# The gate ahead of the reciprocal at the end of an attention group, a third buffer of exponentials, and narrower blocks of ones

## The chip, the cores and the metric

The kernel runs on one core of a Trainium2 chip. The metric is the device time of one execution in microseconds (us); lower is better. The engines are named as the profile names them: PE (matmuls; PEld for its weight loads), DVE (vector), ACT (activations, casts), POOL (the general engine) and SP (the queue that issues most DMAs).

## What is computed

Two layers of a diffusion backbone over 1024 latent tokens and 256 context tokens of 1024 channels. The even layer has two attentions of 8 query heads and 2 key heads each: a global one over all 1280 keys, and a windowed one over the context and a band of +-128 latent keys, with a learned sink per head. The odd layer has a convolution module and a neighbourhood attention of 8 heads on the 16x64 grid with a bias table. Every branch is multiplied by a SiLU gate. What matters here is the end of each attention:

```python
p = jax.nn.softmax(s, axis=-1)                       # with the sink as one more column in the windowed one
o = jnp.einsum("bhgqk,bkhd->bqhgd", p.astype(v.dtype), v)
...
y_lat = jnp.concatenate([oa * jax.nn.silu(ag), ob * jax.nn.silu(bg)], axis=-1) @ w_out     # even layer
y_lat = jnp.concatenate([oc, od * jax.nn.silu(dg)], axis=-1) @ w_out                       # odd layer
```

## The kernel before

All products run on PE as three products of parts: each operand is split into a high part (rounded to the type that PE takes in one pass) and a low part (the rest), as high x high, low x high and high x low. `split` (L323) does it: a cast on ACT, a subtraction on POOL or DVE.

**Order of the work.** Both layers weave two streams: `main`, the attention (`attn_gen`, L428), and a filling of projections (`weave`, L533, with fixed numbers of steps of each). The framework then puts every engine's instructions into an order by these priorities and its own estimate of times; on the chip each engine runs its list in order. So a slow step holds whatever stands behind it on its engine.

**Groups.** In the first layer a group is one unit `u` (of four: 4 query heads that share a key head) and one block of 128 queries (`group0`, L595), so 512 columns of queries x heads; units run in the order 2, 3, 0, 1, blocks in the order `QORD` (2, 3, 4, 0, 5, 6, 1, 7, 8, 9). Blocks 0 and 1 are context and have two key tiles of 128; the others have 4 or 5 (windowed units) or 10 (global ones). In the second layer a group is one head and one half of the grid (`group1`, L1376), with seven key tiles. There are 40 and 16 groups and 364 tiles in all.

**A tile** (L488 to L528): PE makes the scores into a bank `st` of PSUM (two buffers; L503, L507), ACT takes the exponentials into `pf` (L515; in the second layer DVE adds the bias first, L512 and L513), `split` makes `ph` (cast, ACT) and `pl` (POOL, every 12th or 5th tile DVE) of it. `pf` has PFB = 2 buffers, in the first layer under the tag `ost`, which some small tiles of the start share; `ph` and `pl` have four each. Up to three tiles later `flush` (L435) multiplies by the values: three products into the bank `ov` of PSUM, which has one buffer. A key block of the value tile `V` holds 192 columns: 64 low parts, 64 high parts, 64 ones. L445 multiplies columns 64 to 192 by `ph`: rows 0 to 63 of `ov` get the values, rows 64 to 127 all get the sum of exponentials. L446 adds the low parts, L447 does columns 64 to 192 with `pl`, and L450 adds the sink.

**The end of a group** (L451 to L459), all on DVE: two transposes of 32x32 blocks bring the sums from rows 64 to 127 of `ov` to partitions (`r1`; of each block only the first row is used later), the reciprocal is taken (`r8`, L457), and a third transpose of a broadcast spreads it over the columns (`rb`, L458). Then `finish`: in the first layer (L665) two multiplies of `ov` by `rb` into `y` (L669), one multiply of `y` by 0.5 and the gate `gt` (L671), then a DMA to `Od` (L674), or for the last unit a split into the operands of the output projection. `y` has one buffer (YB). In the second layer (L1447) the same with L1451, L1453 and a DMA to `O1d`; its `y1` shares a tag of three buffers with the gate. The gate's rows are loaded by `gate` (L605, L1402) when the middle tile of the group is reached. Only when the last read of `ov` is done may L445 of the next group begin.

`V` is filled by DMA from DRAM (L590, L1410), its ones are set once by POOL for each of the two buffers (L582, L379); at the start the same tag serves as a buffer for modulation weights (`mw_tile`, L168).

Of the kernel before, what the change touches and what calls it, by code (L numbers as in the profile page):

```python
# [10 lines left out]
F32 = mybir.dt.float32  # L11
# [27 lines left out]
VSH = 5  # L39
VORD = (1, 2, 0)  # L40
WBN = 8
TRV = "pp"
HALF = {'half': 3, 'hf': 2}
STG = {"pair": 2, "vT": 1, "spo": 2}
# [3 lines left out]
VS0 = 12  # L48
N0 = 9
NLAST = (48, 28)  # L50
PFB = 2
MWB, WRB = 2, 4
OHQ = 0
PCB = 3
# [46 lines left out]
def tile_kernel(ctx: ExitStack, tc: tile.TileContext, a, out):  # L101
# [23 lines left out]
    def nm(s):  # L125
        uid[0] += 1
        return f"{s}_{uid[0]}"
# [40 lines left out]
    def mw_tile():  # L168

        ring = MWR if mwp[0] is not None else "ABAV"  # L170
        mk[0] += 1
        t = ring[mk[0] % len(ring)]
        if t == "x":
            w = mwp[0].tile([P, 1024], F32, tag="mwx", name=nm("mw"), bufs=2)
        else:
            w = a0.tile([P, 1920 if t == "V" else NTOK], F32, tag={"A": "KA", "B": "KB", "V": "V"}[t], name=nm("mw"),
                        bufs=2)
        return w[:, 0:1024].rearrange("p (d n) -> p d n", d=2)

# [8 lines left out]
    def mod_half(pool, l, part, j):  # L188

        pb = bank("pp", nm("pm"))  # L190
        c0 = part * 1024 + j * 512
        for d2 in range(4):
            w2 = mw_tile()
            mm0.append(SY.dma_start(w2, a["mod_w"][l, 2 * d2 * P : (2 * d2 + 2) * P, c0 : c0 + 512].rearrange("(d p) n -> p d n", d=2)))
            for d in range(2):
                dk = 2 * d2 + d
                pmm.append(PE.matmul(pb[0:2, :], csil[:, dk, :], w2[:, d, :], start=(dk == 0), stop=(dk == DK - 1)))
            yield
        row = a0.tile([P, 512], F32, tag="ost", name=nm("mrow"), bufs=2)[0:2, :]
        SC.copy(row, pb[0:2, :])  # L200
        yield
        tr = bank("tr", nm("trm"))
        for i in range(4):
            PE.transpose(tr[:, 2 * i : 2 * i + 2], row[:, i * P : (i + 1) * P], ident[0:2, 0:2])
        trv = tr[:, 0:8].rearrange("p (i c) -> p i c", c=2)
        o = part * 8 + j * 4
        dst = modT[l][:, o : o + 4, :]
        VE.tensor_tensor(dst, trv, modb[:, l, o : o + 4, None].broadcast_to([P, 4, 2]), op=ALU.add)
        if part == 1:
            VE.scalar_tensor_tensor(gs[l][:, j * 4 : j * 4 + 4, :], dst, 1.0,  # L210
                                    normg[:, l, j * 4 : j * 4 + 4, None].broadcast_to([P, 4, 2]),
                                    op0=ALU.add, op1=ALU.mult)
        yield
# [160 lines left out]
    Ks, Vs = [], []  # L374

    def v_tiles(pool, n, bufs=1):
        Vs[:] = [pool.tile([P, n, 192], F32R, tag="V", name=nm("Vt"), bufs=bufs) for _ in range(bufs)]
        for V in Vs:
            GP.memset(V[:, :, 128:192].bitcast(F32), 1.0)  # L379

    def k_tiles(pool, n, bufs=1):
        KA = pool.tile([P, n * P], F32R, tag="KA", name=nm("KAt"), bufs=bufs)
# [42 lines left out]
    def flat(ap, q, n):  # L425
        return ap[:, :n].rearrange("p (r c) -> p r c", c=q[1]) if isinstance(q, tuple) else ap[:, :n]

    def attn_gen(pool, groups, vshare, look, nexts=None):  # L428

        preps = [g.prep for g in groups]  # L430
# [4 lines left out]
        def flush():  # L435
            g, t, ph, pl = pend.pop(0)
            k, q0, n, _ = g.tiles[t]
            if t == 0:
                g.ov = bank("ov", nm("ov"))
                if g.load_v is not None:  # L440
                    g.load_v()
            V = g.v(k)
            last = t == len(g.tiles) - 1
            o, ph, pl = cut(g.ov, q0, n), flat(ph, q0, n), flat(pl, q0, n)
            PE.matmul(o, V[:, 64:192], ph, start=(t == 0), stop=False)  # L445
            PE.matmul(cut(g.ov[0:64], q0, n), V[:, 0:64], ph, start=False, stop=False)  # L446
            pvs.append(PE.matmul(o, V[:, 64:192], pl, start=False, stop=(last and g.sink is None)))  # L447
            if last:
                if g.sink is not None:
                    PE.matmul(g.ov, g.skm(), g.QL[0:76, :], start=False, stop=True)  # L450
                r1 = pool.tile([P, 8, 32], F32, tag="r1", name=nm("r1"), bufs=1)  # L451
                r8 = pool.tile([P, 8], F32, tag="r8", name=nm("r8"), bufs=2)
                rb = pool.tile([P, 256], F32, tag="rb", name=nm("rb"), bufs=1)
                for e in range(2):
                    VE.transpose(r1[e * 64 : (e + 1) * 64].rearrange("p a b -> p (a b)")
                                 .rearrange("p (a q) -> p a q", a=2), g.den(g.ov[64:128, :], e))
                VE.reciprocal(r8, r1[:, :, 0])  # L457
                VE.transpose(rb, r8[:, :, None].broadcast_to([P, 8, 32]))  # L458
                g.finish(g.ov, rb)  # L459

        for p in preps[:2]:
            if not layer[0]:
# [112 lines left out]
    def kv_tiles(u):  # L575

        if not both:
            for _ in range(2):
                both.append((a0.tile([P, NTOK], F32R, tag="KB", name=nm("KBt"), bufs=2),
                             a0.tile([P, 10, 192], F32R, tag="V", name=nm("Vt"), bufs=2)))  # L580
                GP.memset(both[-1][0][64:68, :].bitcast(F32), 1.0)
                GP.memset(both[-1][1][:, :, 128:192].bitcast(F32), 1.0)  # L582
        KAs[u] = a0.tile([P, NTOK], F32R, tag="KA", name=nm("KAt"), bufs=2)
        KBs[u], V0s[u] = both[ORDER.index(u) % 2]

    def load_kv(u, j0, j1):

        ts = slice(j0 * P, j1 * P)
        SY.dma_start(KAs[u][:, ts].bitcast(F32), Kd[u][:, ts])
        SY.dma_start(V0s[u][:, j0:j1, 0:128].bitcast(F32), Vd[u][:, j0:j1])  # L590

    def copy_k(KA, KB):
        SC.copy(KB[0:64, :], KA[0:64, :].bitcast(F32))
# [1 line left out]
    def group0(u, qb):  # L595
# [66 lines left out]
        def den(dn, e):  # L662
            return dn.rearrange("p (e f q) -> p f e q", f=2, e=2)[:, :, e, :]

        def finish(ov, rb):  # L665
            y = a0.tile([P, 2, P], F32, tag="y", name=nm("y"), bufs=YB)
            for e in range(2):
                es = slice(e * 64, (e + 1) * 64)
                VE.tensor_tensor(y[es], den(ov[0:64, :], e), rb[es, :].rearrange("p (a q) -> p a q", a=2),  # L669
                                 op=ALU.mult)  # L670
            VE.scalar_tensor_tensor(y, y, 0.5, g.gt, op0=ALU.mult, op1=ALU.mult)  # L671
            fs, ts = slice(2 * u, 2 * u + 2), slice(qb * P, (qb + 1) * P)
            if u != ORDER[-1]:
                SY.dma_start(Od[:, fs, ts], y)  # L674
            else:
                c = 0 if qb < 2 else (1 if qb < 6 else 2)
                o = qb * P - CHUNKS[c][0]
                split(y, oh[c][0][:, fs, o : o + P], oh[c][1][:, fs, o : o + P], "s", "v")

        hs = (u - 2) * 4  # L680
        g = Group(load_q=load_q, start=lambda: None, last=last, bias=False, ahead=lambda t: None, rate=3 if isb else 2, gate=gate, v=lambda k: V0s[u][:, k, :], load_v=None, maxes=maxes, nmp=1 if qb < 2 else (2 if isb else 3),
                  sink=(sink[:, hs : hs + 4], sink8[:, hs : hs + 4]) if isb else None, skm=lambda: sk, k=lambda: (KAs[u], KBs[u]),
                  tiles=[(k, 0, 512, x) for k, x in kt], den=den, finish=finish)
        g.prep = attn_prep(kvp, g)
        return g

# [3 lines left out]
    with ExitStack() as p0x:  # L690
# [91 lines left out]
            bmask = const("k_bm", [P, 384], SY, a0)  # L782
        bmt = a0.tile([P, 2, P], F32R, tag="bmt", name="bmt")
        sk = a0.tile([76, P], F32R, tag="sk", name="sk")
        cst = a0.tile([P, 512], F32, tag="ost", name="cst", bufs=2)
        with after_x():
            SY.dma_start(cst[:, 0:256], a["k_bt"].rearrange("p a b -> p (a b)"))
            SY.dma_start(cst[0:76, 256:384], a["k_sk"])
# [20 lines left out]
        def load_g0(u):  # L809

            wh, wl = {}, {}
            for d2 in range(4):
                h_ = a0.tile([P, 2, 256], F32R, tag="ph", name=nm("gh"), bufs=LOOK0 + 1)
                l_ = a0.tile([P, 2, 256], F32R, tag="pl", name=nm("gl"), bufs=LOOK0 + 1)
                raw = a0.tile([P, 2, 256], F32, tag="ost", name=nm("gr"), bufs=2)
                with after_x():
                    SY.dma_start(raw, a["ev_g"][2 * d2 * P : (2 * d2 + 2) * P, u * 256 : (u + 1) * 256]
                                 .rearrange("(d p) n -> p d n", d=2))
# [364 lines left out]
    with ExitStack():  # L1183
# [192 lines left out]
        def group1(gi, hd, hf):  # L1376
# [27 lines left out]
            def start():  # L1404
# [2 lines left out]
                if hf == 0 and hd < 7:  # L1407
                    load_head(hd + 1)
                for j, k, n in ((0, 0, 2), (2, 2 + 5 * hf, 5)):
                    SY.dma_start(Vs[gi % 2][:, j : j + n, 0:128].bitcast(F32), VD[i][:, k : k + n, e])  # L1410

            def last():
                if hf == 0 and hd < 7:
# [30 lines left out]
            def den(dn, k):  # L1444
                return dn[:, k * 256 : (k + 1) * 256].rearrange("p (a q) -> p a q", a=2)

            def finish(ov, rb):  # L1447
                fin[0] += 1
                y = half("y1")
                for k in range(2):  # L1450
                    VE.tensor_tensor(y[ds, k * 256 : (k + 1) * 256], ov[0:64, k * 256 : (k + 1) * 256],  # L1451
                                     rb[k * 64 : (k + 1) * 64, :], op=ALU.mult)
                VE.scalar_tensor_tensor(y[ds], y[ds], 0.5, g.gt[ds], op0=ALU.mult, op1=ALU.mult)  # L1453
                if i == 3:
                    split(y[ds], od3[hf][ds, 0], od3[hf][ds, 1], "s", "v")
                    return
                SY.dma_start(O1d[ds, i, hf], y[ds])

            g = Group(load_q=load_q, maxes=maxes, nmp=2, bias=True, rate=3, ahead=ahead, sink=None, tiles=tiles, den=den, finish=finish,
                      start=start, gate=gate, last=last, load_bs=load_bs,  # L1460
                      k=lambda: Ks[hd % len(Ks)], load_v=None, v=lambda k: Vs[gi % 2][:, k if k < 2 else k - 5 * hf, :])
            g.prep = attn_prep(kvp, g)
            return g

# [338 lines left out]
```

## Time and profile before

| what | value |
|---|---|
| median of 3 runs | 1506.44 us (1504.36 to 1511.38) |
| the profiled execution | 1513.41 us, span in the profile 1511.6 us |
| granted clock of PE over the span | 0.978 |
| busy: PE, DVE, POOL, ACT | 94%, 72%, 54%, 50% |
| attention of the first layer | about 163 to 890 us of the span |
| attention of the second layer | about 1195 to 1480 us |

The profile is of one execution of its own; its times are compared with its own 1513.41 us, not with the median. A row names the line, the engine and the operation, then what is written and read. "[2.19 <-DVE y L669]" at the end of a row of a time line says that the engine had been idle for 2.19 us and that the instruction of L669 on DVE ended that. Busy time of PE counts matmuls whose modelled durations overlap. In a row by source, three numbers with slashes are the least, the median and the largest duration in ns.

### The profile page before, as it was taken

Reading aid. Unit: us, or ns where it says so; the run is one execution under the profiler, and the core shown is the slowest. Engines: PE = TensorE matmul, PEld = TensorE weight load, DVE = VectorE, ACT = ScalarE, POOL = GpSimd, SP = SyncE. Lnnn points to the kernel's source line nnn. Section 1 sums busy time; section 2 is a strip of 40 time slices with the busy share of each in tenths; the row PEclk is TensorE's granted clock in tenths of the full one; section 3 lists DMA queues with packets and bytes.
Section 4 is the critical chain, followed back from the end, with each engine's and each line's share of the span. In section 5 each row is a group of like instructions: output and inputs, shape, how many; then the busy total and the mean of one; then the engine's idle time right before and its main releaser. Section 6 shows DMA issues by size and latency. Waiting matters only on the chain.

```text
span 1511.6 us, 22035 instructions
## 1 busy us (share of the span) xinstructions
PE 1427.4 (94%) x7006; PEld 1162.7 (77%) x7006; DVE 1086.5 (72%) x2139; ACT 750.7 (50%) x1536; POOL 815.9 (54%) x764
## 2 busy tenths in 40 slices
PE   7699999999999999999999989999999999999996
PEld 2598988887788678778888768888887778777775
DVE  4996787588957677555577686999838467667766
ACT  3541444445453765665455665443444354645563
POOL 3262463466555686776455765754543253354663
PEclk9799999999999999999999989999999999999998
DMA  9766245423541124641111122213596777786523
GB/s 350 260 198 194 70 122 179 143 70 115 159 136 48 45 84 120 221 157 38 49 42 43 60 91 66 92 58 80 164 308 189 206 228 207 249 273 209 190 63 119
DMA packets 182828, 215.24 MB, mean 142 GB/s; under 512 B 17196, under 2 KB 136184, under 8 KB 182712
## 3 DMA queue, kind: packets, MB, share of 16 engines
q1 hardware_dynamic: 172464, 195.97, 41.5%
q10 hardware_dynamic: 10248, 17.87, 3.7%
q8 instruction: 55, 0.90, 0.2%
q14 instruction: 61, 0.50, 0.1%
HBM read 151.64 MB, written 62.13 MB: 141 GB/s over the span
## 4 chain that ended last, share of the span: by engine, by line
PE 68%; DVE 13%; DMA 10%; issue 3%; POOL 2%; SPq 1%; ACT 1%; DVEq 0%; ACTq 0%; POOLq 0%
PE p L347 5%; PE p L348 5%; PE p L349 5%; PE ov L445 4%; PE ov L447 4%; PE ov L446 4%; PE po L347 4%; PE po L349 4%; PE po L348 4%; PE st L507 4%; PE st L503 4%; PE pg L347 2%; PE pg L349 2%; PE pg L348 2%; DMA mw<-in_mod_w_dram 2%
## 5 line engine op out<-in xcount | busy, mean ns | idle before, releaser
L328 POOL TENSOR_TENSOR pl<-pf,ph 128x512 fp32r<-128x512 f32 (+3 forms) x321 | 391.6, 1230 | 263.4 <-ACT ph L325 223.1
L328 POOL TENSOR_TENSOR wl<-wr,wh 128x256 fp32r<-128x256 f32 (+2 forms) x253 | 194.9, 789 | 157.5 <-ACT wh L325 114.6
L515 ACT ACTIVATE pf<-st 128x512 f32<-128x512 f32 x284 | 166.9, 596 | 178.4 <-PE st L507 125.6
L325 ACT CAST ph<-pf 128x512 fp32r<-128x512 f32 (+3 forms) x364 | 206.2, 578 | 25.4 <-PE ov L446 12.7
L347 PE MATMUL p<-hh,wh 128*128 128x512 f32 x448 | 177.9, 399 | 4.8 <-ACT wh L325 3.7
L348 PE MATMUL p<-hl,wh 128*128 128x512 f32 x448 | 178.3, 399 | 0.0
L349 PE MATMUL p<-hh,wl 128*128 128x512 f32 x448 | 173.3, 397 | 0.0
L325 ACT CAST wh<-wr 128x256 fp32r<-128x256 f32 (+2 forms) x260 | 102.0, 404 | 122.8 <-DMA wr<-in_od_d_dram 36.3
L445 PE MATMUL ov<-ph,Vt 128*128 128x512 f32 (+3 forms) x364 | 140.6, 386 | 9.5 <-DVE y L669 6.8
L503 PE MATMUL st<-QH,KAt 128*128 128x512 f32 (+3 forms) x364 | 140.3, 386 | 7.5 <-ACT pf L515 4.3
L447 PE MATMUL ov<-pl,Vt 128*128 128x512 f32 (+3 forms) x364 | 141.6, 391 | 4.9 <-POOL pl L328 3.0
L446 PE MATMUL ov<-ph,Vt 128*64 128x512 f32 (+3 forms) x364 | 138.1, 379 | 0.0
L507 PE MATMUL st<-QL,KBt 68*128 68x512 f32 (+3 forms) x364 | 135.1, 381 | 0.3 <-DVE QL L416 0.3
L1200 DVE SCALAR_TENSOR_TENSOR cps<-U,taps,cps 128x512 f32<-128x512 f32 x184 | 124.3, 749 | 0.1
L627 DVE TENSOR_REDUCE mp<-mx 128x1 f32<-128x512 f32 x128 | 85.6, 685 | 38.6 <-PE mx L626 37.9
L347 PEld LDWEIGHTS p<-hh,wh 128*128 128x128 f32 x448 | 84.6, 189 | 25.6 <-ACT wh L325 4.7
L349 PEld LDWEIGHTS p<-hh,wl 128*128 128x128 f32 x448 | 84.4, 189 | 19.7 <-issue 0.5
L348 PEld LDWEIGHTS p<-hl,wh 128*128 128x128 f32 x448 | 84.6, 189 | 18.9 <-issue 0.2
L447 PEld LDWEIGHTS ov<-pl,Vt 128*128 128x128 f32 x364 | 70.3, 193 | 29.5 <-POOL pl L328 7.8
L445 PEld LDWEIGHTS ov<-ph,Vt 128*128 128x128 f32 x364 | 70.7, 194 | 25.1 <-issue 5.3
L503 PEld LDWEIGHTS st<-QH,KAt 128*128 128x128 f32 x364 | 69.1, 190 | 26.3 <-ACT pf L515 10.3
L347 PE MATMUL pq<-wh,hh 128*128 128x384 f32 x256 | 88.7, 346 | 0.0
(289 smaller groups left out, 3463.5 us busy)
## 6 DMA issues: line engine op xcount, KB each, us to landing
mw<-in_mod_w_dram SPq DMA_DIRECT2D x34, 512.0 KB, 6.0
Q<-qs SPq DMA_DIRECT2D x40, 256.0 KB, 2.6
QH<-Q SPq DMA_DIRECT2D x80, 128.0 KB, 2.8
bm<-in_d_bm_dram SPq DMA_DIRECT2D x16, 540.0 KB, 5.9
wr<-in_od_d_dram SPq DMA_DIRECT2D x64, 128.0 KB, 2.9
mw<-in_mod_w_dram SPq DMA_DIRECT2D x28, 256.0 KB, 3.1
wr<-in_ev_qkv_dram SPq DMA_DIRECT2D x32, 192.0 KB, 4.5
QD<-spq SPq DMA_DIRECT2D x48, 128.0 KB, 2.5
```

Of the source, the lines that this page charges most:

```text
L325: SC.copy(hi, src)
L328: (GP if leng == "g" else VE).tensor_tensor(lo, src, hi.bitcast(F32), op=ALU.subtract)
L347: PE.matmul(o, lh, rh, start=first, stop=False)
L348: PE.matmul(o, lh, rl, start=False, stop=False)
L349: done[0] = PE.matmul(o, ll, rh, start=False, stop=last)
L445: PE.matmul(o, V[:, 64:192], ph, start=(t == 0), stop=False)
L446: PE.matmul(cut(g.ov[0:64], q0, n), V[:, 0:64], ph, start=False, stop=False)
L447: pvs.append(PE.matmul(o, V[:, 64:192], pl, start=False, stop=(last and g.sink is None)))
L503: sts.append(PE.matmul(sf, KA[:, cs], cut(g.QH, q0, n), start=True, stop=False))
L507: PE.matmul(sf, KB[0:68, cs], cut(g.QL[0:68], q0, n), start=False, stop=True)
L515: SC.activation(pf[:, :n], st[:, :n], AF.Exp, scale=1.0 if g.bias else SCALE)
L1200: VE.scalar_tensor_tensor(pc, uc, w, pc, op0=ALU.mult, op1=ALU.add)
```

## The change

- At the end of a group the gate comes first: a new `pre` multiplies `ov` by 0.5 and the gate, two instructions of 64 rows x 256 columns, placed right behind the two transposes. Reciprocal and third transpose follow, and `finish` multiplies by `rb` out of SBUF: one instruction in the first layer, two in the second. In the first layer `pre` writes `y`; in the second it writes a new tile `yu` of one buffer.
- PFB goes from 2 to 3, for both layers and for what shares the tag.
- A key block of `V` has VW = 161 columns: 64 low, 64 high, 33 ones. The products L445 and L447 then have 97 columns. The first product of a group keeps 128, to write all rows of `ov`; its last 31 columns are the next block's low parts, and a pad of 31 ones stands behind the last block. Rows 97 to 127 of `ov` are not used.
- The ones are set by one memset for each key block and one for the pad: 11 for a tile of ten blocks, 8 for one of seven.

The core of the diff:

```diff
-PFB = 2
+PFB = 3
+VW = 161
...
+    def new_v(pool, n, bufs):
+
+        V = pool.tile([P, n * VW + 192 - VW], F32R, tag="V", name=nm("Vt"), bufs=bufs)
+        for k in range(n):
+            GP.memset(V[:, k * VW + P : (k + 1) * VW].bitcast(F32), 1.0)
+        GP.memset(V[:, n * VW :].bitcast(F32), 1.0)
+        return V
+
+    def v_keys(V):
+        return V[:, : V.shape[1] // VW * VW].rearrange("p (k d) -> p k d", d=VW)
...
-            PE.matmul(o, V[:, 64:192], ph, start=(t == 0), stop=False)
-            PE.matmul(cut(g.ov[0:64], q0, n), V[:, 0:64], ph, start=False, stop=False)
-            pvs.append(PE.matmul(o, V[:, 64:192], pl, start=False, stop=(last and g.sink is None)))
+            m = P if t == 0 else VW - 64
+            PE.matmul(o[0:m], V[:, vo + 64 : vo + 64 + m], ph, start=(t == 0), stop=False)
+            PE.matmul(cut(g.ov[0:64], q0, n), V[:, vo : vo + 64], ph, start=False, stop=False)
+            pvs.append(PE.matmul(o[0 : VW - 64], V[:, vo + 64 : vo + VW], pl, start=False, stop=(last and g.sink is None)))
...
+                yu = g.pre(g.ov)
                 VE.reciprocal(r8, r1[:, :, 0])
                 VE.transpose(rb, r8[:, :, None].broadcast_to([P, 8, 32]))
-                g.finish(g.ov, rb)
+                g.finish(yu, rb)
...
-        def finish(ov, rb):
+        def pre(ov):
             y = a0.tile([P, 2, P], F32, tag="y", name=nm("y"), bufs=YB)
             for e in range(2):
                 es = slice(e * 64, (e + 1) * 64)
-                VE.tensor_tensor(y[es], den(ov[0:64, :], e), rb[es, :].rearrange("p (a q) -> p a q", a=2),
-                                 op=ALU.mult)
-            VE.scalar_tensor_tensor(y, y, 0.5, g.gt, op0=ALU.mult, op1=ALU.mult)
+                VE.scalar_tensor_tensor(y[es], den(ov[0:64, :], e), 0.5, g.gt[es], op0=ALU.mult, op1=ALU.mult)
+            return y
+
+        def finish(y, rb):
+            VE.tensor_tensor(y, y, rb.rearrange("p (a q) -> p a q", a=2), op=ALU.mult)
...
+            def pre(ov):
+                yu = dpool.tile([P, 256], F32, tag="yu", name=nm("yu"), bufs=1)
+                for k in range(2):
+                    VE.scalar_tensor_tensor(yu[k * 64 : (k + 1) * 64], ov[0:64, k * 256 : (k + 1) * 256], 0.5,
+                                            g.gt[ds, k * 256 : (k + 1) * 256], op0=ALU.mult, op1=ALU.mult)
+                return yu
+
+            def finish(yu, rb):
                 fin[0] += 1
                 y = half("y1")
                 for k in range(2):
-                    VE.tensor_tensor(y[ds, k * 256 : (k + 1) * 256], ov[0:64, k * 256 : (k + 1) * 256],
+                    VE.tensor_tensor(y[ds, k * 256 : (k + 1) * 256], yu[k * 64 : (k + 1) * 64],
                                      rb[k * 64 : (k + 1) * 64, :], op=ALU.mult)
-                VE.scalar_tensor_tensor(y[ds], y[ds], 0.5, g.gt[ds], op0=ALU.mult, op1=ALU.mult)
```

The other lines of the diff follow from these: `v` hands back the tile and the number of the block, the DMAs go through `v_keys`, and the size of the shared buffers is adapted.

More of the change, by code (lines that the diff above doesn't have):

```diff
@@ L175, in mw_tile @@
         else:
-            w = a0.tile([P, 1920 if t == "V" else NTOK], F32, tag={"A": "KA", "B": "KB", "V": "V"}[t], name=nm("mw"),
+            w = a0.tile([P, 10 * VW + 192 - VW if t == "V" else NTOK], F32, tag={"A": "KA", "B": "KB", "V": "V"}[t], name=nm("mw"),
                         bufs=2)
@@ L198, in mod_half @@
             yield
-        row = a0.tile([P, 512], F32, tag="ost", name=nm("mrow"), bufs=2)[0:2, :]
+        row = a0.tile([P, 512], F32, tag="ost", name=nm("mrow"), bufs=PFB)[0:2, :]
         SC.copy(row, pb[0:2, :])
@@ L376, in v_tiles @@
     def v_tiles(pool, n, bufs=1):
-        Vs[:] = [pool.tile([P, n, 192], F32R, tag="V", name=nm("Vt"), bufs=bufs) for _ in range(bufs)]
-        for V in Vs:
-            GP.memset(V[:, :, 128:192].bitcast(F32), 1.0)
+        Vs[:] = [new_v(pool, n, bufs) for _ in range(bufs)]
     def k_tiles(pool, n, bufs=1):
@@ L441, in flush @@
                     g.load_v()
-            V = g.v(k)
+            V, vo = g.v(k)
+            vo *= VW
             last = t == len(g.tiles) - 1
             o, ph, pl = cut(g.ov, q0, n), flat(ph, q0, n), flat(pl, q0, n)
-            PE.matmul(o, V[:, 64:192], ph, start=(t == 0), stop=False)
-            PE.matmul(cut(g.ov[0:64], q0, n), V[:, 0:64], ph, start=False, stop=False)
-            pvs.append(PE.matmul(o, V[:, 64:192], pl, start=False, stop=(last and g.sink is None)))
+            m = P if t == 0 else VW - 64
+            PE.matmul(o[0:m], V[:, vo + 64 : vo + 64 + m], ph, start=(t == 0), stop=False)
+            PE.matmul(cut(g.ov[0:64], q0, n), V[:, vo : vo + 64], ph, start=False, stop=False)
+            pvs.append(PE.matmul(o[0 : VW - 64], V[:, vo + 64 : vo + VW], pl, start=False, stop=(last and g.sink is None)))
             if last:
@@ L579, in kv_tiles @@
                 both.append((a0.tile([P, NTOK], F32R, tag="KB", name=nm("KBt"), bufs=2),
-                             a0.tile([P, 10, 192], F32R, tag="V", name=nm("Vt"), bufs=2)))
+                             new_v(a0, 10, 2)))
                 GP.memset(both[-1][0][64:68, :].bitcast(F32), 1.0)
-                GP.memset(both[-1][1][:, :, 128:192].bitcast(F32), 1.0)
         KAs[u] = a0.tile([P, NTOK], F32R, tag="KA", name=nm("KAt"), bufs=2)
@@ L589, in load_kv @@
         SY.dma_start(KAs[u][:, ts].bitcast(F32), Kd[u][:, ts])
-        SY.dma_start(V0s[u][:, j0:j1, 0:128].bitcast(F32), Vd[u][:, j0:j1])
+        SY.dma_start(v_keys(V0s[u])[:, j0:j1, 0:128].bitcast(F32), Vd[u][:, j0:j1])
     def copy_k(KA, KB):
@@ L680, in group0 @@
         hs = (u - 2) * 4
-        g = Group(load_q=load_q, start=lambda: None, last=last, bias=False, ahead=lambda t: None, rate=3 if isb else 2, gate=gate, v=lambda k: V0s[u][:, k, :], load_v=None, maxes=maxes, nmp=1 if qb < 2 else (2 if isb else 3),
+        g = Group(load_q=load_q, start=lambda: None, last=last, bias=False, ahead=lambda t: None, rate=3 if isb else 2, gate=gate, v=lambda k: (V0s[u], k), load_v=None, maxes=maxes, nmp=1 if qb < 2 else (2 if isb else 3),
                   sink=(sink[:, hs : hs + 4], sink8[:, hs : hs + 4]) if isb else None, skm=lambda: sk, k=lambda: (KAs[u], KBs[u]),
-                  tiles=[(k, 0, 512, x) for k, x in kt], den=den, finish=finish)
+                  tiles=[(k, 0, 512, x) for k, x in kt], den=den, pre=pre, finish=finish)
         g.prep = attn_prep(kvp, g)
@@ L784, in tile_kernel @@
         sk = a0.tile([76, P], F32R, tag="sk", name="sk")
-        cst = a0.tile([P, 512], F32, tag="ost", name="cst", bufs=2)
+        cst = a0.tile([P, 512], F32, tag="ost", name="cst", bufs=PFB)
         with after_x():
@@ L814, in load_g0 @@
                 l_ = a0.tile([P, 2, 256], F32R, tag="pl", name=nm("gl"), bufs=LOOK0 + 1)
-                raw = a0.tile([P, 2, 256], F32, tag="ost", name=nm("gr"), bufs=2)
+                raw = a0.tile([P, 2, 256], F32, tag="ost", name=nm("gr"), bufs=PFB)
                 with after_x():
@@ L1409, in start @@
                 for j, k, n in ((0, 0, 2), (2, 2 + 5 * hf, 5)):
-                    SY.dma_start(Vs[gi % 2][:, j : j + n, 0:128].bitcast(F32), VD[i][:, k : k + n, e])
+                    SY.dma_start(v_keys(Vs[gi % 2])[:, j : j + n, 0:128].bitcast(F32), VD[i][:, k : k + n, e])
             def last():
@@ L1457, in finish @@
                 SY.dma_start(O1d[ds, i, hf], y[ds])
-            g = Group(load_q=load_q, maxes=maxes, nmp=2, bias=True, rate=3, ahead=ahead, sink=None, tiles=tiles, den=den, finish=finish,
+            g = Group(load_q=load_q, maxes=maxes, nmp=2, bias=True, rate=3, ahead=ahead, sink=None, tiles=tiles, den=den, pre=pre, finish=finish,
                       start=start, gate=gate, last=last, load_bs=load_bs,
-                      k=lambda: Ks[hd % len(Ks)], load_v=None, v=lambda k: Vs[gi % 2][:, k if k < 2 else k - 5 * hf, :])
+                      k=lambda: Ks[hd % len(Ks)], load_v=None, v=lambda k: (Vs[gi % 2], k if k < 2 else k - 5 * hf))
             g.prep = attn_prep(kvp, g)
```

1 line of the change is left out of this document (removed).

## The prediction

> **What bounds the kernel now.** I read the page first: its first part says which engine has no room.
>
> ```profile
> PE 1427.4 (94%) x7006; PEld 1162.7 (77%) x7006; DVE 1086.5 (72%) x2139; ACT 750.7 (50%) x1536; POOL 815.9 (54%) x764
> ```
>
> PE is busy for 1427.4 of 1511.6 us, so a change that leaves PE's matmuls as they are can only win what PE loses by waiting. The next view is therefore the waits of PE (total, times, longest), from which these lines touch the change:
>
> ```profile
> PE ov L445 <- DVE y L669: 6.8, 6, 2.2
> PE st L503 <- ACT pf L515: 4.3, 9, 1.2
> ...
> PE ov L447 <- POOL pl L328: 3.0, 8, 0.8
> ```
>
> The first is the one buffer of `ov` in PSUM: the next group's first product with the values waits until the group end on DVE has read the old sums. The second is PE waiting for a free bank of scores, because ACT has not yet taken the exponentials. The third is the split of the exponentials on POOL, which the change leaves alone. The time line of PE shows the three long cases of the first:
>
> ```profile
> 380.62 0.51 PE L445 MATMUL ov<-ph,Vt 128*128 128x512 f32 x1 [2.19 <-DVE y L669]
> ...
> 550.62 0.49 PE L445 MATMUL ov<-ph,Vt 128*128 128x512 f32 x1 [1.90 <-DVE y L669]
> ...
> 864.79 0.60 PE L445 MATMUL ov<-ph,Vt 128*128 128x512 f32 x1 [1.89 <-DVE y L669]
> ```
>
> 2.19 + 1.90 + 1.89 = 5.98 of the 6.8 us; the other three are 0.8 us together. Why DVE was late is in its own time line:
>
> ```profile
> 374.07 0.92 DVE L455 STREAM_TRANSPOSE r<-ov 64x256 f32<-64x256 f32 x2
> ...
> 546.06 0.92 DVE L455 STREAM_TRANSPOSE r<-ov 64x256 f32<-64x256 f32 x2
> ...
> 862.13 0.92 DVE L455 STREAM_TRANSPOSE r<-ov 64x256 f32<-64x256 f32 x2 [1.80 <-PE ov L447]
> 863.08 0.20 DVE L457 RECIPROCAL r<-r 128x8 f32<-128x8 f32 x1
> 863.32 0.45 DVE L458 STREAM_TRANSPOSE rb<-r 128x256 f32<-128x256 f32 x1
> 863.80 0.85 DVE L669 TENSOR_TENSOR y<-ov,rb 64x256 f32<-64x256 f32 x2
> ```
>
> In the third group the six instructions that hold `ov` follow each other without a break: 862.13 to 864.65, 2.5 us. In the first two, other work stands between them: the transposes began at 374.07 and 546.06, yet PE was let go only at 380.6 and 550.6, that is 6.5 and 4.5 us later. Each of the dependent steps (reciprocal, second transpose, multiply) left a gap into which another instruction was put.
>
> **Part 1, the group end.** The two transposes stay first. The gate multiply now reads `ov` directly behind them, two instructions of 64x256, and `ov` is free after those; reciprocal, second transpose and the multiply by it read nothing from PSUM. The trace has no gate multiply out of PSUM, so its price is that of the nearest rows (min/median/max in ns):
>
> ```profile
> L669 DVE TENSOR_TENSOR y<-ov,rb x80: 396/417/421, 182.3 to 888.6; 64x256 f32<-64x256 f32 x80
> L671 DVE SCALAR_TENSOR_TENSOR y<-y,gt x40: 410/426/1501, 183.3 to 889.7; 128x256 f32<-128x256 f32 x40
> ...
> L1453 DVE SCALAR_TENSOR_TENSOR y<-y,gt x16: 673/690/1707, 1219.7 to 1480.0; 64x512 f32<-64x512 f32 x16
> ```
>
> L669 reads the same PSUM rows at 417 ns, L671 is the same operation on as many columns at 426; I take 0.42 us, 0.84 for two, and the bounds 0.40 and 0.43 change nothing. So `ov` is free 0.92 + 0.84 = 1.8 us after the transposes begin, against at least 2.5. Now the three long waits. First: free at 374.07 + 1.8 = 375.9, while PE came to it at 380.62 - 2.19 = 378.4: all 2.19 us go. Second: free at 547.9, PE came at 548.7: all 1.90 go. Third: free at 863.9 instead of 864.65: 0.7 of 1.89 goes. The three short ones, 0.8 us, go wholly, since each end gets at least 0.7 us shorter. Sum 5.6 us, with 3.4 below (only the second, the third's part and the short ones) and 6.8 above.
>
> A wait costs more than itself where the granted clock falls behind it (columns: stretch, length, busy time of PE, PEld, DVE, ACT, POOL, granted clock, DMA):
>
> ```profile
> 376.00:380.00 4.00, 2.43 (x16) 2.10 (x14) 3.97 (x8) 0.95 (x3) 3.24 (x5) 1.00 0.62 191
> 380.00:384.00 4.00, 3.38 (x15) 2.40 (x15) 3.89 (x6) 1.43 (x5) 4.00 (x5) 1.00 0.27 82
> 384.00:388.00 4.00, 2.99 (x17) 2.31 (x16) 3.89 (x10) 3.97 (x10) 3.65 (x4) 1.00 0.29 72
> 551.00:555.00 4.00, 4.00 (x12) 2.87 (x11) 1.74 (x3) 2.66 (x5) 3.56 (x5) 0.58 0.31 93
> 865.00:869.00 4.00, 4.00 (x12) 2.82 (x12) 1.80 (x2) 3.04 (x6) 3.15 (x3) 0.58 0.00 0
> ```
>
> Behind the second and third wait the clock was 0.58 for 4 us: 4 x 0.42 = 1.7 us of matmuls lost each time, though behind the first it stayed at 1.00. The second loss goes with its wait; of the third, whose wait is only cut to 1.2 us, I count half. 1.7 + 0.85 = 2.5 us, with 0 and 3.4 as bounds. The Trainium skill (TensorE: Matmul & The Clock Gate, Part 1: The HAM clock gate) says that the clock is halved after an idle window of about 3.4 us. By that rule waits of 2 us cost no clock, and this term would be 0, the sum 6.5 us. The trace speaks against it: 0.58 stands right behind waits of 1.9 us.
>
> The rows of the stretch from 376 to 388 also show DVE at 3.97, 3.89 and 3.89 of 4 us. What PE gains there, DVE cannot follow: I keep half of the 2.19 us and take 1.1 off.
>
> Else in this part: the gate's rows were loaded half a group earlier and nothing on DVE waits for them in the trace; a group of the first layer keeps its three DVE multiplies. In the second layer a gate multiply of 64x512 (0.69 us) becomes two multiplies of 64x256 out of SBUF; at 0.43 each that is 0.17 us more for each of 16 groups, 2.7 us of DVE (below: 0.1 each, above: 1.0, the slowest of L671). It costs PE nothing while DVE, at 72%, has room; the reciprocal comes 0.84 us later, and only in the last group does that lengthen anything, by the same 0.17 us.
>
> **Part 2, the third buffer of exponentials.** ACT's idle time before the exponentials, by what ended it:
>
> ```profile
>   PE st L507: 125.6, 83
>   POOL pl L328: 37.0, 44
>   DVE pl L328: 5.0, 5
> ```
>
> The last two are the reuse of a `pf` buffer: the split of two tiles ago still reads it. They are 42.0 of 167.6 us, a quarter. PE waited for ACT here 4.3 us, and its weight loads as well:
>
> ```profile
> PEld st L503 <- ACT pf L515: 10.3, 19, 1.4
> ```
>
> A quarter of 4.3 is 1.1 us, a quarter of 4.3 + 10.3 is 3.6. I take 2.0, nearer to PE's own row, because part of a load's wait is covered by the matmul before it. The lower bound is 0: the third tile can be exponentiated sooner, but its split still queues on POOL. What is late next is then that split, the 3.0 us of L447.
>
> **Part 3, the narrow ones.** A weight tile of 97 columns (64 and 33) takes the place of one of 128, in 672 of the products with the values (two for each of 364 tiles, less the first of each of 40 + 16 groups). What the number of columns does, 128 in L445 and 64 in L446, is in the rows of `ov`:
>
> ```profile
> L445 PEld LDWEIGHTS ov<-ph,Vt x364: 186/188/333, 168.0 to 1473.2; 128*128 128x128 f32 x182
> L445 PE MATMUL ov<-ph,Vt x364: 221/390/792, 168.2 to 1473.3; 128*128 128x512 f32 x142, 128*128 128x384 f32 x16, 128*128 128x256 f32 x16, 128*128 128x128 f32 x8
> L446 PEld LDWEIGHTS ov<-ph,Vt x364: 133/134/232, 168.2 to 1473.4; 128*64 128x64 f32 x182
> L446 PE MATMUL ov<-ph,Vt x364: 220/393/628, 168.4 to 1473.6; 128*64 128x512 f32 x142, 128*64 128x384 f32 x16, 128*64 128x256 f32 x16, 128*64 128x128 f32 x8
> ```
>
> The load gets shorter (134 against 188 ns), the matmul does not (393 against 390): loads run beside the matmul before. I take 0. The first product of a group still has 128 columns, 31 of them the next block's; both blocks come with one DMA, so nothing new is waited for.
>
> The ones are set block by block, 11 small memsets for 1 in the first layer's tile, 8 for 1 in the second's, two tiles each.
>
> ```profile
> L1034 POOL MEMSET U<- 128x15 f32 x4 | 0.4, 114 | 0.0
> ```
>
> A block of 33 lies between one such row and three: 38 x 0.11 to 38 x 0.34, 4 to 13 us of POOL less what the four old memsets took, all ahead of the attention, where POOL (54%) has room. I count nothing, and 1 us if that cover is gone.
>
> **Sum.** 5.6 + 2.5 + 2.0 - 1.1 = 9.0 us. The profiled execution took 1513.4 us, 7.0 above the median of 1506.4 shown, so 1513.4 - 9.0 = 1504.4 for its like and 1506.4 - 9.0 = 1497.4 for a median. The ends of the terms give 3.4 - 1.1 + 0 + 0 = 2.3 and 6.8 + 3.4 + 3.6 = 13.8, with the 3.0 us of L447 at most 16.8: 1489.6 to 1504.1.
>
> **Rivals.** *The next wait takes it over* (1506). For: DVE near 3.9 of 4 us in the stretch of the longest wait, and a PE order that is made anew around each group end. Against: at 551 DVE had 1.74 of 4 us to do, so at least the second wait has nothing behind it. Gain within 3 us either way, 1503.4 to 1509.4.
>
> *The single `y` buffer makes DVE wait* (slower). `y` is now written by the gate multiply, right behind the transposes, so it must be free that much earlier; in the first three units of the first layer it is free only when its DMA to `Od` has landed. One such DMA in SP's time line, and the landings of all 30:
>
> ```profile
> 408.77 0.38 SPq L674 DMA_DIRECT2D Od<-y  x1
> ```
>
> ```profile
> DMA to landing us min/median/max: 1.8/1.8/5.8
> ```
>
> The end of the group behind it, one of two key tiles, in DVE's time line:
>
> ```profile
> 410.79 0.92 DVE L455 STREAM_TRANSPOSE r<-ov 64x256 f32<-64x256 f32 x2
> ```
>
> Its transposes are done at 411.71, 1.1 us after the earliest landing at 410.57. If the shorter hold of `ov` brings that group's sums over 1.1 us nearer, DVE stands at the multiply, and the maxima, the score splits and the rotary work queue behind it. From a landing of 3 us on, that is 1 to 4 us of DVE in each of the 6 two-tile groups and in those behind them, where DVE has no room: some 6 x 2 = 12 us of DVE, 8 of it on PE if little of part 1 is gained: 1514. Against: most groups are 5 or 10 tiles apart, and the old multiply into `y` needed the same landing only 0.7 us later.
>
> *The loads count* (1489). 672 loads x 31/64 of 54 ns = 17.6 us, if the loads and not the matmuls set PE's pace. The rows of L445 and L446 speak against it. The Trainium skill (TensorE: Matmul & The Clock Gate, LDWEIGHTS) lets a load grow with its columns alone, which the 134 and 188 ns bear out, but not that it is on the path.
>
> **How the numbers follow.** Forecast 0.58, taken over 0.23, `y` 0.14, loads 0.05. A run of this kernel can tell about 0.5%, 7.5 us, from no change: of the forecast's 0.58 some 0.43 lies beyond that, so faster is 0.43 + 0.05 = 0.48, slower is 0.13 of the `y` case, the same is 0.39. The range goes from the loads' 1488 to 1511, where the second rival ends and the third begins; past it lies most of the 0.14.
>
> **What would show it.** Right: no wait of L445 for DVE over 1.5 us, no 0.58 behind one, the gate multiply next to the transposes on DVE, ACT's waits for POOL before the exponentials under half of 37 us, matmuls of L445 and L447 near 390 ns. Wrong: DVE idle at the gate multiply for the `Od` DMA; the waits of L447 or of the scores' maxima grown by what L445 lost; PE's total of waits as before.

## The result and the profile after

| | before | after |
|---|---|---|
| median, us (lowest to highest) | 1508.12 of 8 runs (1504.36 to 1512.04) | 1500.17 of 8 runs (1496.98 to 1502.72; one at 1743.68) |
| the profiled execution, us | 1513.41 | 1498.59 |
| its span, us, and clock | 1511.6, 0.978 | 1496.8, 0.982 |

The ratio is 0.9944 with a 95% interval of 0.9926 to 0.9962: 0.56% faster, about 8 us, where 9.0 had been forecast. The run of 1743.68 us had a mean granted clock of 0.746 over its span and is left out of the comparison. The two profiled executions lie 14.8 us apart, 6.9 more than the medians: that of before was 5.3 us above its median, that of after 1.6 below.

The page of after, its first part:

```profile
span 1496.8 us, 22043 instructions
...
PE 1418.6 (95%) x7006; PEld 1149.4 (77%) x7006; DVE 1091.0 (73%) x2155; ACT 744.4 (50%) x1536; POOL 813.7 (54%) x798
```

The span less PE's busy time was 1511.6 - 1427.4 = 84.2 us and is 78.2. The clock took 1511.6 x 0.022 = 33 us and takes 1496.8 x 0.018 = 27. So some 6 of the 14.8 us are idle time and some 6 are clock. DVE has 4.5 us more to do. Its multiplies at the group ends alone take 6.6 us more: 2.7 in the second layer and 3.9 in the first, where the multiply by `rb` out of SBUF (L685) takes 0.69 us in the mean against 0.60 for L671 before. POOL has 34 instructions more and is no busier.

The waits of PE (total, times, longest), those that answer to the lines of before and two more:

```profile
PE mx L1438 <- DMA KAt<-KD: 6.2, 2, 3.7
...
PE ov L457 <- DVE y L681: 2.8, 4, 1.0
PE ov L457 <- DVE yu L1464: 2.4, 1, 2.4
...
PE ov L459 <- POOL pl L329: 2.1, 3, 1.0
...
PE st L516 <- ACT pf L528: 1.4, 4, 0.6
```

The wait for the group end was 6.8 us and is 2.8 + 2.4 = 5.2: only 1.6 of the 5.6 us went. The scores' wait for the exponentials fell by 2.9, from 4.3 to 1.4, and the split's by 0.9. Two more rows have to be read with them, here from the waits of PE in the kernel before:

```profile
PE st L503 <- DVE pf L512: 2.8, 4, 0.9
...
PE mx L1424 <- DMA KAt<-KD: 1.0, 1, 1.0
```

Both are of the second layer. The wait of the scores' bank for the bias on DVE, 2.8 us, is not in the list of after at all. The wait for the keys of the next head has grown from 1.0 to 6.2. They lie in other places (the keys at 1215 and 1288 us, the bias at 1320 to 1442), so that the one takes back what the other gave is not shown. All waits at the products for the scores' maxima (`mx`) together have grown as well, from 9.4 to 16.2 us: 5.2 more for the keys and 3.6 more for the queries of the first layer, while those for DVE's work on the maxima fell from 6.7 to 3.6.

The group end itself does what the arithmetic said. One in DVE's time line:

```profile
856.36 0.92 DVE L467 STREAM_TRANSPOSE r<-ov 64x256 f32<-64x256 f32 x2 [1.33 <-PE ov L459]
857.31 0.85 DVE L681 SCALAR_TENSOR_TENSOR y<-ov,gt 64x256 f32<-64x256 f32 x2
858.18 0.20 DVE L470 RECIPROCAL r<-r 128x8 f32<-128x8 f32 x1
858.42 0.45 DVE L471 STREAM_TRANSPOSE rb<-r 128x256 f32<-128x256 f32 x1
858.90 0.69 DVE L685 TENSOR_TENSOR y<-y,rb 128x256 f32<-128x256 f32 x1
```

`ov` is free at 858.16, 1.8 us after the transposes begin. Over all 56 ends of the time line that time was 3.9 us in the median before, and is 1.8. Yet the longest wait is 2.45 us, where it was 2.19. Its place, first in PE's time line and then in DVE's:

```profile
1425.26 0.47 PE L459 MATMUL ov<-pl,Vt 128*97 128x512 f32 x1
1425.72 0.45 PE L516 MATMUL st<-QH,KAt 128*128 128x384 f32 x1
1426.00 0.34 PE L520 MATMUL st<-QL,KBt 68*128 68x384 f32 x1
1428.79 0.76 PE L457 MATMUL ov<-ph,Vt 128*128 128x512 f32 x1 [2.45 <-DVE yu L1464]
```

```profile
1425.70 0.68 DVE L415 TENSOR_TENSOR QL<-trn,k_bd 4x512 fp32r<-4x512 f32 x1
1426.41 0.29 DVE L329 TENSOR_TENSOR pl<-pf,ph 128x128 fp32r<-128x128 f32 x1
1426.74 0.92 DVE L467 STREAM_TRANSPOSE r<-ov 64x256 f32<-64x256 f32 x2
1427.68 0.85 DVE L1464 SCALAR_TENSOR_TENSOR yu<-ov,gt 64x256 f32<-64x256 f32 x2
```

The hold is as short as it can be, 1426.74 to 1428.53, and nothing stands in it. But PE had finished its work at 1426.34, before the transposes began: the next group's product stands two matmuls behind the last one, with too little work between them to cover even 1.8 us. The transposes add to it, since they come 1.0 us after the end of that last product (1425.73), behind two other instructions of DVE. That PE's next product has moved nearer holds for the group ends as a whole. Counted in the traces, a median of 35 to 38 other matmuls stands between a group's last product with the values and the next group's first in the seven kernels of this document without the new end, and 25 to 28 in the seven with it. Ends with less than 3 us of PE's work there number 2 or 3 without it and 8 to 14 with it. So the order made anew with the shorter hold has used much of it up. The windows around this wait (busy time of PE, PEld, DVE, ACT, POOL, then granted clock):

```profile
1426.00:1430.00 4.00, 1.55 (x5) 0.91 (x5) 3.81 (x10) 1.37 (x4) 1.17 (x2) 0.79 0.33 97
1430.00:1434.00 4.00, 4.00 (x15) 3.33 (x15) 3.01 (x5) 3.00 (x8) 2.30 (x3) 0.50 0.00 0
```

Behind it the clock is 0.50 for the whole of the next 4 us. The Trainium skill (TensorE: Matmul & The Clock Gate, Part 1: The HAM clock gate) puts such a drop behind an idle window of about 3.4 us; here a drop followed a wait of 2.45 us, as it followed waits of 1.9 us in the kernel before.

The third buffer shows in the idle time of ACT ahead of the exponentials of the first layer, by what ended it, and in who waited for them:

```profile
  PE st L520: 127.2, 103
  POOL pl L329: 12.0, 10
...
  DVE pl L329: 2.6, 3
...
  PEld st L516: 4.9, 12
...
  PE st L516: 1.4, 4
```

37.0 + 5.0 us of waits for a buffer have become 12.0 + 2.6; PE's loads waited 10.3 us for the exponentials and wait 4.9. The remaining waits of ACT are for scores, so for PE.

The narrow loads, by source:

```profile
L457 PEld LDWEIGHTS ov<-ph,Vt x364: 160/163/288, 163.2 to 1458.9; 128*97 128x97 f32 x140, 128*128 128x128 f32 x42
L457 PE MATMUL ov<-ph,Vt x364: 220/392/763, 163.4 to 1459.0; 128*97 128x512 f32 x100, 128*128 128x512 f32 x42, 128*97 128x384 f32 x16, 128*97 128x256 f32 x16
```

The median load went from 188 to 163 ns, the median matmul from 390 to 392.

### The profile page after: what moved, and what is told of

Read it like the earlier page. It is cut to its first block, busy times and chain, and to the rows that moved or that the text cites. A ratio compares the mean times of both kernels' runs of the same rounds, so it can differ in the third digit from the quotient of the medians.

```text
span 1496.8 us, 22043 instructions
## 1 busy us (share of the span) xinstructions
PE 1418.6 (95%) x7006; PEld 1149.4 (77%) x7006; DVE 1091.0 (73%) x2155; ACT 744.4 (50%) x1536; POOL 813.7 (54%) x798
## 4 chain that ended last, share of the span: by engine, by line
PE 78%; DVE 9%; DMA 7%; issue 3%; POOL 1%; ACT 1%; SPq 0%; ACTq 0%; DVEq 0%; POOLq 0%
PE p L348 7%; PE p L349 7%; PE p L350 7%; PE ov L457 4%; PE st L520 4%; PE ov L459 4%; PE po L348 4%; PE po L350 4%; PE po L349 4%; PE st L516 4%; PE ov L458 4%; PE pq L348 3%; PE pq L349 3%; PE pq L350 3%; DMA mw<-in_mod_w_dram 2%
## 5 line engine op out<-in xcount | busy, mean ns | idle before, releaser
L329 POOL TENSOR_TENSOR wl<-wr,wh 128x256 fp32r<-128x256 f32 (+2 forms) x253 | 191.8, 776 | 149.3 <-ACT wh L326 120.6
L457 PE MATMUL ov<-ph,Vt 128*97 128x512 f32 (+4 forms) x364 | 139.2, 383 | 8.4 <-ACT ph L326 3.1
L459 PE MATMUL ov<-pl,Vt 128*97 128x512 f32 (+3 forms) x364 | 139.3, 384 | 2.8 <-POOL pl L329 2.1
L349 PE MATMUL pq<-wl,hh 128*128 128x384 f32 x256 | 88.1, 344 | 0.0
L350 PE MATMUL pq<-wh,hl 128*128 128x384 f32 x256 | 87.8, 343 | 0.0
```

Of the source, the lines that this page charges most:

```text
L329: (GP if leng == "g" else VE).tensor_tensor(lo, src, hi.bitcast(F32), op=ALU.subtract)
L349: PE.matmul(o, lh, rl, start=False, stop=False)
L350: done[0] = PE.matmul(o, ll, rh, start=False, stop=last)
L457: PE.matmul(o[0:m], V[:, vo + 64 : vo + 64 + m], ph, start=(t == 0), stop=False)
L459: pvs.append(PE.matmul(o[0 : VW - 64], V[:, vo + 64 : vo + VW], pl, start=False, stop=(last and g.sink is None)))
```

## The experiments

The change has three parts, and the question was which of them the 8 us come from. Theory 1 is that of the prediction: most comes from the shorter hold, and the parts add up. Theory 2: the third buffer alone brings it. Theory 3: the narrow loads do. Theory 4: none of them; the framework puts the instructions into another order whenever a line is touched, and the time follows the order. Each ratio below is against the kernel before on the same chip.

**Parts alone.** The new group end without the other two, from the kernel after:

```diff
-VW = 161
+VW = 192
-PFB = 3
+PFB = 2
...
-        GP.memset(V[:, n * VW :].bitcast(F32), 1.0)
```

> The gate ahead of the reciprocal alone: two buffers of exponentials, blocks of 64 ones as before. Theory 1 (the shorter hold of the PSUM bank of the sums is most of the gain, the third buffer the rest, narrow blocks nothing): 5.6 + 2.5 - 1.1 = 7 us faster than before, ratio about 0.995, and the bank free 1.8 us after the first transpose in most groups. Theory 2 (the third buffer is the gain): no change, ratio 1.000. Theory 3 (shorter weight loads are the gain): no change. Theory 4 (any edit shuffles the order of the work and that is the gain): anything within 6 us, not the sum of parts.

Measured: 1523.45 us, ratio 1.0107 (1.0079 to 1.0136). Slower by 15 us where 7 were to be won. All of the change but the third buffer:

```diff
-PFB = 3
+PFB = 2
```

> The whole change but with two buffers of exponentials. Theory 1: 7 us faster than before, 2 us slower than the whole change; ACT's waits for POOL ahead of the exponentials stay near 37 us. Theory 2: no change against before. Theory 3: the whole 8 us. Theory 4: not to be told from the parts.

Measured: 1524.34 us, ratio 1.0108 (1.0080 to 1.0137). The third buffer and the narrow blocks, with the old group end (`pre` goes, `finish` as before):

```diff
-                yu = g.pre(g.ov)
...
-                g.finish(yu, rb)
+                g.finish(g.ov, rb)
```

> Three buffers of exponentials and narrow blocks of ones, the group end as before. Theory 1: 2 us faster than before (ratio 0.9987), ACT's waits for POOL ahead of the exponentials down to a half or less, the waits of the values' product for DVE as before near 7 us. Theory 2: 8 us faster. Theory 3: 8 us faster. Theory 4: anything within 6 us.

Measured: 1514.62 us, ratio 1.0046 (1.0027 to 1.0065). The narrow blocks alone, from the kernel before:

```diff
+VW = 161
...
-            PE.matmul(o, V[:, 64:192], ph, start=(t == 0), stop=False)
+            m = P if t == 0 else VW - 64
+            PE.matmul(o[0:m], V[:, vo + 64 : vo + 64 + m], ph, start=(t == 0), stop=False)
```

> Narrow blocks of ones alone: two buffers, the group end as before. Theory 1: no change, ratio 1.000 within 0.002, loads of 97 columns near 163 ns, matmuls near 390 ns. Theory 2: no change. Theory 3: 8 us or more faster. Theory 4: up to 6 us either way, which would then be the size of what a mere change of order does.

Measured: 1522.23 us, ratio 1.0109 (1.0079 to 1.0139). Theory 2 is out, since the third buffer without the new end loses as well. Theory 3 is out: shorter loads gained nothing, and the new end is at 1523.4 us with wide blocks and at 1524.3 with narrow ones. So is theory 1 as it stood, since the new group end alone loses. But that every part is slower than before, also the one that only shortens loads, is hardly an effect of the parts. It points to theory 4, though theory 4 had allowed 6 us and 6 to 16 came. In the kernel with the new end alone PE's waits are these:

```profile
PE ov L456 <- DVE yu L1463: 6.1, 3, 3.4
PE ov L456 <- DVE y L680: 5.1, 4, 1.5
```

11.2 us where before has 6.8, although `ov` is free 1.8 us (median) after the transposes here too.

**Another order.** To tell parts from orders, the four kernels (none of the parts, new end, third buffer, all) were run with an edit that has nothing to do with them: one small copy on DVE, at about 59 us of the span, is made in two pieces. It adds one short instruction, and the order of all engines differs from there on: PE's list from 77 us, and in the kernel before it has the same tiles at 70% of its 7006 places. The narrow blocks are in all but the first.

```diff
-        VE.tensor_copy(sk, cst[0:76, 256:384])
+        VE.tensor_copy(sk[0:64, :], cst[0:64, 256:384]), VE.tensor_copy(sk[64:76, :], cst[64:76, 256:384])
```

> The kernel before with one small copy near 85 us made in two, which does no work that counts but makes the framework order much of the rest anew. Theory 1 (parts add up: hold and third buffer) and theory 5 (the hold pays only together with the third buffer): 1508 within 3 us. Theory 4 (order alone decides, and the orders of before and after are lucky ones): near the 1514 to 1524 of the partial versions, 8 to 15 us slower than before.

Measured: 1522.97 us, ratio 1.0107 (1.0078 to 1.0137).

> The gate first and narrow blocks, two buffers, with the same small copy in two. Theory 1: 7 us faster than the reordered kernel before. Theory 5: again near 1524. Theory 4: anywhere from 1505 to 1527, not tied to the 1524 of its first order.

Measured: 1524.38 us, ratio 1.0106 (1.0079 to 1.0132).

> Three buffers and narrow blocks, the old group end, with the same small copy in two. Theory 1: 2 us faster than the reordered kernel before. Theory 5: near 1514. Theory 4: anywhere from 1505 to 1527.

Measured: 1515.33 us, ratio 1.0043 (1.0023 to 1.0062).

> The whole change with the same small copy in two. Theory 1: 9 us faster than the reordered kernel before, near 1500. Theory 5: near 1500, with the other three well above. Theory 4: well above 1500, among the others.

Measured: 1511.02 us, ratio 1.0016 (1.0000 to 1.0031).

The copy in two pieces costs the kernel before 15 us and the kernel after 11; the other two move by less than 1. So the order can be worth more than any part, but it is not all: with the copy in two the four still differ. Theory 5 of these expectations, parts that pay only together, had the kernel before at 1508 and the whole change near 1500, and missed both. **A third set of orders** was made to see whether the ranks stay. This time a cast on ACT, which runs 20 times, is cut in two (ACT is busy 4 us more). The theory stated for it, number 6, was that the third buffer brings about 8 us in any order, the new end nothing without it and 4 or more with it, and that the order of the kernel before is worth some 15.

```diff
-                SC.copy(vs[:, :, 1], pc[:, :, 320:384])
+                SC.copy(vs[:, 0, 1], pc[:, 0, 320:384]), SC.copy(vs[:, 1, 1], pc[:, 1, 320:384])
```

> The kernel before with another harmless edit that makes the framework order the work anew (a small cast of ACT in two, 20 times, 4 us of ACT that has room). Theory 6 (an order of its own is worth about 15 us to the kernel before, the third buffer about 8 us in any order, the gate nothing without and some 4 us or more with the third buffer): 1522 within 4 us. Theory 1 (parts add, order does not matter): 1508. Theory 4 (order alone): anywhere from 1500 to 1527.

Measured: 1523.28 us, ratio 1.0107 (1.0084 to 1.0131).

> The gate first and narrow blocks, two buffers, with the cast in two. Theory 6: 1524 within 3 us, no faster than the kernel before with the same edit; the bank of the sums free 1.8 us after the first transpose, and PE's waits for it no shorter than before. Theory 1: 7 us faster than that kernel. Theory 4: anywhere from 1500 to 1527.

Measured: 1523.72 us, ratio 1.0106 (1.0064 to 1.0147).

> Three buffers and narrow blocks, old group end, with the cast in two. Theory 6: 1515 within 3 us, about 8 us faster than the kernel before with the same edit. Theory 1: 2 us faster than that. Theory 4: anywhere from 1500 to 1527.

Measured: 1512.34 us, ratio 1.0036 (1.0023 to 1.0050).

> The whole change with the cast in two. Theory 6: between 1500 and 1511, the fastest of the four, and the fewest microseconds of clock lost. Theory 1: 9 us faster than the kernel before with the same edit. Theory 4: not the fastest of the four but by chance.

Measured: 1506.37 us, ratio 0.9988 (0.9967 to 1.0009).

The medians together, in us:

| | no such edit | copy in two | cast in two |
|---|---|---|---|
| none of the parts | 1508.1 | 1523.0 | 1523.3 |
| narrow blocks alone | 1522.2 | | |
| new end (with narrow blocks) | 1524.3 | 1524.4 | 1523.7 |
| third buffer, narrow blocks | 1514.6 | 1515.3 | 1512.3 |
| all | 1500.2 | 1511.0 | 1506.4 |

A column shares an edit, not an order: each kernel's order is its own. In PE's lists, the four kernels of one of the last two columns have the same tiles at 37 to 51% of the places, the kernels of one row at 55 to 83%. So what counts is whether a row lies apart from another in all columns. Down each of the last two columns the third buffer (with the narrow blocks) brings 7.6 and 10.9 us, and in the first, from the narrow blocks alone, 7.6. The new end by itself costs 1.4 and 0.4 (nothing that can be told from zero), and added to the third buffer it brings 4.3 and 6.0; from the third buffer alone to all it is 14.4 in the first column. The times of theory 6 held in all four kernels. One of its signs did not: the whole change was to lose the fewest microseconds of clock, and with the cast in two its granted clock was 0.972 to 0.980 over ten runs, that of the third buffer alone 0.978 to 0.983. The kernel before is the one that falls out: of the eight kernels with two buffers of exponentials, seven lie between 1522 and 1525, and it at 1508.

What the parts do to ACT, in the waits of ACT for a buffer of exponentials (`pf`) and of their cast (`ph`), all with the cast in two. None of the parts, new end, third buffer, all:

```profile
ACT pf L515 <- POOL pl L328: 38.5, 47, 3.2
ACT ph L325 <- PE ov L446: 20.7, 16, 3.3
...
ACT pf L515 <- DVE pl L328: 7.0, 7, 2.2
```

```profile
ACT pf L528 <- POOL pl L329: 26.0, 31, 3.1
...
ACT pf L528 <- DVE pl L329: 3.1, 4, 1.2
...
ACT ph L326 <- PE ov L458: 2.3, 3, 1.3
```

```profile
ACT pf L527 <- POOL pl L329: 21.8, 20, 4.8
ACT ph L326 <- PE ov L458: 14.0, 20, 2.5
...
ACT pf L527 <- DVE pl L329: 1.7, 2, 1.1
```

```profile
ACT pf L528 <- POOL pl L329: 10.8, 11, 2.7
ACT ph L326 <- PE ov L458: 9.4, 11, 2.0
```

ACT is held in two places, one on each side of the tile: at `pf`, until the split two or three tiles back is done, and at `ph`, until PE has multiplied an older tile by the values. The new end frees the second (20.7 to 2.3) and part of the first (45.5 to 29.1), the third buffer mostly the first (45.5 to 23.5), and both together leave 10.8 and 9.4. In the other columns it is much the same: 41.6 to 42.9 us at `pf` with neither, 29.8 to 38.7 with the new end, 25.2 and 27.3 with the third buffer, 11.4 and 14.6 with both. That fits a gain that needs both, but it doesn't prove it: by the sum of these rows the new end alone (31.4) should be ahead of the third buffer alone (37.5), and it is 11 us behind.

## Why the prediction came out right, and where its steps did not

**The total** held, 8 against 9.0 us, but not by its terms, and the agreement is luck. With the copy and the cast in two the whole change brings 12.0 and 16.9 us. Without such an edit it brings less because the kernel before has a good order, 15 us better than its two neighbours, and the kernel after a good one too, 6 and 11 us better. The prediction took the order as given and counted nothing for it. Of its signs of being right, three came (the gate multiply behind the transposes, ACT's waits, the matmuls) and two did not: a wait of 2.45 us for the group end remains, with a clock of 0.50 behind it. One sign of being wrong came as well, the grown waits at the scores' maxima, 6.8 us more.

**5.6 us of waits for the group end.** This step failed. Its first half was right to the number: 0.417 us for the gate multiply out of PSUM and 1.8 us from the transposes to a free `ov`, in 43 of the 56 ends. The second half, that PE would come to it at the same time as before, was not: some ten matmuls fewer stand in between. Without the new end the seven kernels wait 3.3 to 8.5 us for a group end, with it 5.0 to 11.2. Two of the rows, of no part and of the new end, both with the cast in two, from the waits of PE:

```profile
PE ov L445 <- DVE y L669: 3.3, 3, 1.9
```

```profile
PE ov L457 <- DVE yu L1464: 5.0, 3, 2.2
...
PE ov L457 <- DVE y L681: 4.2, 5, 1.4
```

What goes reliably is the second layer's wait of the scores for the bias on DVE: 2.4 to 4.6 us in the seven kernels without the new end, 0.0 to 0.3 in the seven with it. What comes, in six of these seven, is the wait for the next head's keys, 3.5 to 6.6 us against 0 to 1.0. That is what the first rival said, that the next wait takes over, within a forecast whose total held; it would explain that the new end by itself brings nothing. That PE's next product moves nearer is counted in all fourteen traces; that the framework's estimate does it is inferred, and no order was held fixed to test it.

**2.5 us of clock.** The loss over the span went from 33 to 27 us, by more than forecast, but only in part for the reason given. The two drops that were named did go: the clock is 1.00 from 551 to 555 and from 857 to 869 us, 1.7 us each. The rest is a balance of other drops, with new ones behind the waits for keys at 1215 and 1288 and behind the group end at 1428.79. How far one run can be trusted here shows in the profiled run of all parts with the cast in two: its clock was 0.972, and its time 8 us above the median of that kernel.

**2.0 us for the third buffer.** This term was mis-sized: 7.6 to 10.9 us where it is added to the old group end, past its upper bound of 3.6 and past the 6.6 with the split's waits. It was priced by PE's waits that name ACT, and those do not even shrink when the buffer comes alone (4.7 us without it and 6.4 with it, with the cast in two). Its gain lies in many small waits and in the clock: in that pair the span less PE's busy time falls from 90.3 to 83.5 us, the lost clock from 37 to 29. The sign that was named, ACT's waits for POOL under half of 37, came true at 12.0. Added to the new end the buffer brings more still, 13.4 to 24.2 us.

**1.1 us off for a full DVE**: not told apart by any run. **Narrow loads at nothing**: right; 188 to 163 ns, the matmul unchanged, 1524.3 us against 1523.4 with the new end, and 1522.2 alone against 1523.0 and 1523.3 for the kernel before with the copy and the cast in two. **Memsets at nothing**: right; the 38 together take 2.8 us of POOL, less than the 4 to 13 that were estimated.

**The single `y` buffer.** The rival was there, and small. DVE stood idle for the `Od` DMA once, for 0.7 us. Three times, at ends of two-tile groups, the order of DVE's list did what the DMA was expected to: the gate multiply was put behind the earlier group's last multiply. In DVE's time line:

```profile
365.30 0.92 DVE L467 STREAM_TRANSPOSE r<-ov 64x256 f32<-64x256 f32 x2
...
366.93 0.41 DVE L685 TENSOR_TENSOR y<-y,rb 128x256 f32<-128x256 f32 x1
...
371.03 0.84 DVE L681 SCALAR_TENSOR_TENSOR y<-ov,gt 64x256 f32<-64x256 f32 x2
```

`y` is in use until its own multiply at 366.93 and the store behind it, and `ov` is held until 371.87, 6.6 us instead of 1.8. PE came to its next product of values only at 373.74 here, so this long hold cost nothing. A second buffer for `y` was not tried.

**What stays open**: why the kernel before has an order 15 us better than its neighbours, and where the 4 to 14 us lie that the new end brings once the third buffer is there. From the third buffer alone to all parts, with the copy in two, PE's idle time rises from 85.3 to 87.1 us and the clock falls from 0.979 to 0.978 while the span falls by 7.3. What falls is PE's busy time, from 1429.8 to 1420.7. Less the lost clock it falls by 10.5 us there and by 10.5 with the cast in two, and by 2.2 without such an edit. Since the profile counts the modelled, overlapping durations of matmuls as busy, short stalls can hide in that number. A count from the traces, at full clock and without the listed idle time, shows them: the starts of the matmuls lie further apart than the first quartile for their shape by 82.3 us in sum with the third buffer alone (copy or cast in two), and by 73.9 and 72.6 with all parts. So part of the gain is in stalls too short to be listed as waits; the shorter waits of ACT would explain them, but no run shows it.

## What to carry to other kernels

Where a framework orders the instructions by its own estimate, a wait that is made shorter can be spent again by the new order: here the next use stood nearer in seven kernels of seven. So price such a wait at little, and look also for a buffer whose reuse holds an engine at many tiles. Before a difference of 1% or less is put down to an edit, both kernels should be run in one or two other orders, made by an edit that does nothing: here this moved two of four kernels by 6 to 15 us and the other two by less than 2.5, and a part was told from chance only where its row lay apart from another under every edit. Parts that are worth nothing alone may be worth something together, so a part is taken away from the whole as well as added to nothing.

## What the runs showed of the hardware

A wait of PE of 2.45 us was followed by a clock of 0.50 for over 4 us, the matmuls of 512 columns then being spaced about 0.43 us apart instead of 0.23. In the clock's records of the fourteen traces, from 150 us on, there are 119 such drops, all to 0.50, all beginning on a grid of 3.413 us that runs through the whole trace, and lasting one to four of its steps; a step costs 1.7 us. What goes with a drop is less the length of one wait than PE's idle time in sum within a step: of 58 steps at full clock with 1.9 us or more of it, 56 were followed by a drop, of 199 with 1.0 to 1.9 us 60, of 5141 with less 3. Taking the span less PE's idle time and lost clock, 1387 to 1398 us are left in all fourteen kernels, so that the times from 1497 to 1526 us of the profiled spans are for the most part a matter of idle time (78 to 93 us) and clock (27 to 46 us); the rest is 1387 to 1392 in the three kernels with all parts and 1394 to 1398 in the three with the third buffer alone. A weight load of 97 columns took 163 ns against 188 for 128, and the matmuls beside it did not get faster. In the kernel after, the multiply of `y` by `rb` out of SBUF, 426 ns in the median, took up to 2457 ns, while the multiplies out of PSUM stayed at 378 to 421 in every kernel.
